# The up projections of a feed-forward layer by seven products of half blocks, in a phase of their own, in a tuned Trainium2 kernel

## The chip, the cores and the metric

The kernel runs on one core of one Trainium2 chip, in one launch. Its time is the device time of that core in microseconds (us), and less is better. The core has a tensor engine (PE, with its weight loads as PEld), VectorE (DVE), ScalarE (ACT), GpSimd (POOL) and a queue engine that issues loads (SP); each works through its own instructions in order and waits for the others by semaphores.

## The reference

One layer of a hybrid backbone on 640 tokens (128 of a prompt, 512 latent) of 2048 features, in float32: four groups of mixers behind a common input projection, an output projection, then a gated feed-forward part of 5632 = 44 x 128 features. The change touches that last part and the modulation ahead of it:

```python
def modulation(cond, w_ada, b_ada):
    m = jax.nn.silu(cond) @ w_ada + b_ada
    return jnp.split(m[:, None, :], N_MOD, axis=-1)

def ffn_sublayer(x, shift, scale, gate, g_pre, g_post, w1, w3, w2):
    h = modulate(rms_norm(x, g_pre), shift, scale)
    y = (jax.nn.silu(h @ w1) * (h @ w3)) @ w2
    return x + gate * rms_norm(y, g_post)
```

## The kernel before

Every large product is made in float32 precision from three float32r products: each operand is split into a rounded part (hi, or Rh, gh) and the rest (lo, or Rl, gl), and hi x hi, hi x lo and lo x hi are summed in PSUM. The input's parts Rh and Rl stay resident, 16 feature blocks by 640 tokens each. Weights come through the class `Stream` (lines 40 to 130): loads of 512 KB into four `raw` buffers on the SP queue run ahead, ScalarE makes the hi part of each half load (L101), VectorE the lo part (L102), both ahead of the products, as far as `part` buffers allow.

The order of all engines is the order in which the program is written: lists of steps (`p_c0`, `p_c1`, `p_wo`, `p_x`, `p_y`, `ff`) are run one after the other, and generators in `fillers` (norms, attention, the chains of the norm ahead of the feed-forward) are advanced by one piece after each step. From the end of the output projection on (tile `wo`, steps `p_wo`):

- `chain_a(t)` finishes the residual of a tile of 128 tokens (`mix`), writes it to DRAM (`x2d`), squares it and makes the diagonal `dg`; `chain_b(t)` transposes it by 16 products with `dg` (tile `tp`), scales and shifts it on ScalarE (L1261) and splits it into Rh and Rl. Three tiles' chains run among the last steps of the output projection, two among the first up products.
- `ff1_step(f, which, kh)` makes an up product for one block of 128 features and one of the weights w1 and w3: per block k of the 16, three passes, each in a matmul of 384 columns (tile `h_...X`) and one of 256 (`h_...Y`) with the weight part stationary (`gemm_b`). For w1 a silu follows on ScalarE, for w3 the multiply on VectorE and the split of the gated block into `gh`, `gl`.
- `ff2_step(c, n, kg)` makes the down product of a chunk of four blocks (11 chunks) for 512 output features: per block and token tile three matmuls of 512 columns with `gh` or `gl` stationary (tile `f`, in the last half chunk `f2l`), then a sum into `acc` (L1035).
- `gate_steps` makes the gates' modulation rows from 32 loads of 512 KB each (tile `gate`, 32 stationary columns): the first set among the input projection, the second threaded among the up products, in bursts of two blocks.

The list `ff` alternates: the first up products of chunk c, the down product of chunk c-1, the other up products of c. After the last chunk `final(t)` norms and writes each tile.

## Time and profile before

| | |
|---|---|
| time, median of 3 runs | 2931.72 us (2927.12 to 2933.48) |
| span of the profiled execution, first to last instruction | 2919.9 us (11.8 under that median; the rest of its own time lies around the span) |
| busy: PE, PEld | 97%, 86% |
| busy: DVE, ACT, POOL | 39%, 30%, 9% |
| mean granted clock of the tensor engine | 0.987 of full speed |
| moved by DMA | 357.99 MB, mean 123 GB/s |

Shares are means over stages with different limits. Matmuls overlap each other, so a matmul's own duration is longer than its share of the tensor engine: the distance from one start to the next is what it costs there. Clocks are given as a part of full speed; 1.00 is 2.4 GHz and 0.50 is 1.2 GHz.

### The profile page before, as it was taken

The page shows a single profiled execution, that of the slowest core. Times are in us where ns is not written, and L with a number is a line of the kernel's source. Part 1 is how long each engine was busy: PE and PEld are TensorE (multiplying, and loading weights), DVE is VectorE, ACT ScalarE, POOL GpSimd, SP SyncE. Part 2 cuts the span into 40 slices and gives each one's busy share as a digit, 9 for nine tenths or more (in the row PEclk, how much of TensorE's full clock was granted, in tenths as well). Part 3 has the DMA queues.
Part 4 walks back from the last instruction along what each step waited for, and adds up shares of the span by engine and source line. Part 5 has one row for each costly group of instructions (what it writes and reads, how often), then busy time and mean ns, then how long its engine had stood idle before and what let it go on. Part 6 is the DMA issues. An engine that isn't in the chain of part 4 may idle for free.

```text
span 2919.9 us, 41605 instructions
## 1 busy us (share of the span) xinstructions
PE 2820.1 (97%) x17244; PEld 2511.4 (86%) x17244; DVE 1147.4 (39%) x1974; ACT 866.6 (30%) x1787; POOL 255.2 (9%) x305
## 2 busy tenths in 40 slices
PE   5999999799999999999999999999999999999997
PEld 3888787678788899898999989899898989989895
DVE  4338955355524842223232232323323232232326
ACT  3235535244423742321221212122121122212124
POOL 0107811210000210000000000000000000000004
PEclk8999999899999999999999999999999999999998
DMA  7965554644333732222222222222222222222224
GB/s 294 317 223 174 191 194 140 124 160 164 115 105 128 253 125 80 86 89 73 102 73 87 87 87 91 76 94 80 87 87 80 94 77 90 87 73 75 77 73 195
DMA packets 103262, 357.99 MB, mean 123 GB/s; under 512 B 12240, under 2 KB 12496, under 8 KB 101408
## 3 DMA queue, kind: packets, MB, share of 16 engines
q1 hardware_dynamic: 94496, 320.38, 32.5%
q0 software_dynamic: 8144, 34.65, 3.4%
q8 instruction: 135, 2.21, 0.3%
q14 instruction: 55, 0.45, 0.0%
q10 hardware_dynamic: 432, 0.30, 0.0%
HBM read 336.37 MB, written 18.91 MB: 122 GB/s over the span
## 4 chain that ended last, share of the span: by engine, by line
PE 71%; DVE 2%; ACT 1%; issue 0%; POOL 0%; DVEq 0%; ACTq 0%
PE f L152 20%; PE wo L152 7%; PE gate L152 1%; PE h_18X L152 1%; PE h_26X L152 1%; PE h_22X L152 1%; PE h_34X L152 1%; PE h_6X L152 1%; PE h_14X L152 1%; PE h_30X L152 1%; PE h_10X L152 1%; PE h_13X L152 1%; PE h_17X L152 1%; PE h_21X L152 1%; PE h_33X L152 1%; PE h_29X L152 1%
## 5 line engine op out<-in xcount | busy, mean ns | idle before, releaser
L102 DVE TENSOR_TENSOR lo<-raw,hi 128x512 fp32r<-128x512 f32 (+1 forms) x800 | 554.9, 699 | 1490.0 <-ACT hi L101 1471.5
L101 ACT CAST hi<-raw 128x512 fp32r<-128x512 f32 (+1 forms) x800 | 477.1, 604 | 1494.5 <-PE f L152 424.9
L152 PE MATMUL f<-lo,gh 128*128 128x512 f32 x840 | 331.8, 395 | 0.0
L152 PE MATMUL f<-hi,gh 128*128 128x512 f32 x840 | 331.8, 395 | 0.0
L152 PE MATMUL f<-hi,gl 128*128 128x512 f32 x840 | 331.8, 395 | 0.0
L152 PEld LDWEIGHTS f<-hi,gl 128*128 128x128 f32 x840 | 157.7, 188 | 38.3
L152 PEld LDWEIGHTS f<-lo,gh 128*128 128x128 f32 x840 | 157.7, 188 | 37.9
L152 PEld LDWEIGHTS f<-hi,gh 128*128 128x128 f32 x840 | 157.7, 188 | 37.8
L357 POOL DMA_DIRECT2D gd<-gm x4 | 2.3, 589 | 1451.7 <-DVE gm L354 1451.7
L152 PE MATMUL wo<-hi,RhG 128*128 128x512 f32 x320 | 128.0, 400 | 0.0
L152 PE MATMUL wo<-lo,RhG 128*128 128x512 f32 x320 | 126.7, 396 | 0.7 <-DVE lo L102 0.7
L152 PE MATMUL wo<-hi,RlG 128*128 128x512 f32 x320 | 126.8, 396 | 0.0
L668 POOL TENSOR_TENSOR side<-side,tap 128x116 f32<-128x116 f32 (+19 forms) x140 | 115.3, 835 | 60.6 <-ACT tap L666 53.5
L1035 DVE TENSOR_TENSOR acc<-f,acc 128x512 f32<-128x512 f32 x190 | 117.1, 679 | 0.0
L152 PE MATMUL ada<-raw,cs 128*32 128x256 f32 x1024 | 75.8, 413 | 24.8 <-DMA raw<-in_w_mod_dram 24.7
L662 DVE SCALAR_TENSOR_TENSOR cm<-u,vec,cm 128x497 f32<-128x497 f32 (+14 forms) x100 | 92.4, 924 | 7.2 <-ACT cm L654 5.1
L1018 ACT CAST gh<-si 128x640 fp32r<-128x640 f32 x44 | 32.1, 729 | 171.2 <-DVE si L1015 171.2
L152 PEld LDWEIGHTS ada<-raw,cs 128*32 128x32 f32 x1024 | 27.1, 113 | 55.0 <-ACT sq L1165 19.5
L152 PEld LDWEIGHTS wo<-lo,RhG 128*128 128x128 f32 x320 | 60.2, 188 | 15.2 <-DVE lo L102 1.2
L152 PEld LDWEIGHTS wo<-hi,RhG 128*128 128x128 f32 x320 | 60.2, 188 | 14.3 <-issue 0.4
L152 PEld LDWEIGHTS wo<-hi,RlG 128*128 128x128 f32 x320 | 60.1, 188 | 14.3
L666 ACT ACTIVATE tap<-u,vec 128x116 f32<-128x116 f32 (+19 forms) x140 | 57.1, 436 | 23.1 <-POOL side L668 21.5
(1618 smaller groups left out, 7109.8 us busy)
## 6 DMA issues: line engine op xcount, KB each, us to landing
raw<-in_w_dram SPq DMA_DIRECT2D x272, 512.0 KB, 3.6
raw<-in_w_mod_dram SPq DMA_DIRECT2D x128, 512.0 KB, 5.2
raw<-in_w_gate_dram SPq DMA_DIRECT2D x64, 512.0 KB, 3.3
raw<-in_w_in_dram SPq DMA_DIRECT2D x64, 384.0 KB, 3.7
raw<-in_w_out_dram SPq DMA_DIRECT2D x48, 512.0 KB, 3.3
raw<-in_w_in_dram SPq DMA_DIRECT2D x16, 512.0 KB, 7.6
ud<-u POOLq DMA_DIRECT2D x24, 320.0 KB, 7.8
u<-ud SPq DMA_DIRECT2D x24, 320.0 KB, 4.2
```

Of the source, the lines that this page charges most:

```text
L101: self.nc.scalar.copy(hi[:, 0:n], t)
L102: self.nc.vector.tensor_tensor(out=lo[:, 0:n], in0=t, in1=f32(hi[:, 0:n]), op=ALU.subtract)
L152: nc.tensor.matmul(out=out, lhsT=lhsT, rhs=rhs, start=start, stop=stop)
L357: nc.gpsimd.dma_start(out=gd[row, cond].rearrange("(q x) -> q x", q=4), in_=dst[cond:P:32, :])
L662: nc.vector.scalar_tensor_tensor(out=o[:, so], in0=x[:, si], scalar=w[:, 15 + d:16 + d], in1=o[:, so], op0=ALU.mult, op1=ALU.add)
L666: nc.scalar.activation(out=t[:, 0:m - abs(d)], in_=x[:, si], func=AF.Copy, scale=w[:, 15 + d:16 + d])
L668: nc.gpsimd.tensor_tensor(out=side[:, so], in0=side[:, so], in1=t[:, 0:m - abs(d)], op=ALU.add)
L1018: nc.scalar.copy(gh[f], s)
L1035: nc.vector.tensor_tensor(out=acc[t][:, cc], in0=b, in1=acc[t][:, cc], op=ALU.add)
```

## The change

The up projections, 640 tokens x 2048 features x 256 output features at a time (a pair p of feature blocks, for w1 and then w3: 44 units), are written as products of 2 x 2 blocks: tokens in two halves of 320 (`TH`), the 16 feature blocks in even and odd ones (eight each, `KP`), the two output blocks. Strassen's seven products (`NP`) replace the eight: `TOKENS` and `WEIGHTS` say which blocks are added or subtracted for each. The sums of the tokens are made and split once (`ch`, `cl`, resident), those of the weights for each unit (`weight_sum`, `weight_low`), each product is 24 matmuls of 320 columns into a bank `m`, and `gather` adds it into the quadrants of the result. The up products run in a loop of their own, with the parts made two products ahead. The gated pair is written to DRAM (`ggd`); the down products, in chunks of 8, 8, 8, 8, 8 and 4 blocks, read it back and split it there (`g_load`, `g_split`). The chains of the norm now leave the scaled tokens unsplit in two tiles, `hal[0]` ("ha") and `hal[1]` ("hb"); once the token sums are made, parts of hb hold weight blocks and a result. The second set of gates is made between the output projection and the up phase, and each gate item covers 256 columns of all four row groups.

```diff
-CF = 4
-NC = NFF // CF
+TH = T // 2
+KP = KD // 2
+CHUNKS = (8, 8, 8, 8, 8, 4)
+NC = len(CHUNKS)
...
+    ggd = dram.tile([NFF // 2, P, 2, T], F32, name="ggd")
...
-        return (a["w_gate"][m // 3, half, k], (1024,), False)
+        return (a["w_gate"][m // 3, half, k], (4, 256), False)
...
-                for j in range(2):
-                    q = 2 * half + j
-                    mm(b[32 * q:32 * q + 32, :], cs[:, k, :], g[:, 512 * j:512 * j + 512],
-                       k % burst == 0, k % burst == burst - 1)
+                for q in range(4):
+                    mm(b[32 * q:32 * q + 32, 0:256], cs[:, k, :], g[:, q, :], k == 0, k == KD - 1)
...
-        return [one(k, half) for k in range(KD) for half in range(2)]
+        return [one(k, half) for half in range(2) for k in range(KD)]
...
-    def ff1_step(f, which, kh, part="XY"):
...
+    NP = 7
+    TOKENS = (((0, 0), (1, 1), ALU.add), ((0, 1), (1, 1), ALU.subtract), ((0, 0), None, None),
+              ((1, 0), (0, 0), ALU.subtract), ((0, 0), (0, 1), ALU.add), ((1, 1), None, None),
+              ((1, 0), (1, 1), ALU.add))
+    WEIGHTS = (((0, 0), (1, 1), ALU.add, False), ((1, 0), (1, 1), ALU.add, False), ((0, 1), (1, 1), ALU.subtract, False),
+               ((0, 1), (0, 0), ALU.add, True), ((1, 1), None, None, True), ((1, 0), (0, 0), ALU.subtract, True),
+               ((0, 0), None, None, True))
+    BLOCKS = ((0, 0), (1, 1), (1, 0), (0, 1))
...
+    N_W, N_HI = 5, 3
...
+    def load_weights(upto=None):
+        while at["load"] < min(4 * len(units), upto or 9999):
+            if upto is None and len(room["extra"]) + min(room["most"] - room["plain"], N_W - room["w"]) < 2:
+                return
+            u_, b_ = divmod(at["load"], 4)
+            p, wh = units[u_]
+            kf = BLOCKS[b_]
+            got = slot(f"B{kf[0] + 1}{kf[1] + 1}_{wh}_{p}", own=upto is not None and kf[1] == 0)
+            assert got is not None, "no room for a block"
+            nc.sync.dma_start(out=got[0], in_=(w1 if wh == 0 else w3)[p, kf[0], kf[1]])
+            raw[u_, kf] = got
+            at["load"] += 1
...
+    def weight_sum(s):
+        u_, i = divmod(s, NP)
+        x, y, op, last = WEIGHTS[i]
+        for kf in (x, y):
+            if kf is not None and (u_, kf) not in raw:
+                load_weights()
+                assert (u_, kf) in raw, ("no room for a block", s, room, list(raw))
+        bx = raw[u_, x]
+        t = bx
+        if y is not None:
+            if not last:
+                t = slot(f"t{i}_{u_}")
+                assert t is not None, "no room for a sum"
+            nc.vector.tensor_tensor(out=t[0], in0=bx[0], in1=raw[u_, y][0], op=op)
+        if last:
+            raw.pop((u_, x))
+        hi = slot(f"hi{i}_{u_}", F32R, "hi")
+        nc.scalar.copy(hi[0], t[0])
+        half[s] = (t, hi)
...
+    def weight_low(s):
+        t, hi = half.pop(s)
+        u_, i = divmod(s, NP)
+        lo = slot(f"lo{i}_{u_}", F32R)
+        assert lo is not None, "no room for a part"
+        nc.vector.tensor_tensor(out=lo[0], in0=t[0], in1=f32(hi[0]), op=ALU.subtract)
+        give(t)
+        held[s] = (hi, lo)
...
+    def product(s):
+        u_, i = divmod(s, NP)
+        hi, lo = held.pop(s)
+        b = bk[u_, i] = bank(f"m{i}_{u_}")
+        o = b[:, 0:TH]
+        for j in range(KP):
+            mm(o, hi[0][:, j, :], ch[i][:, j, :], j == 0, False)
+            mm(o, hi[0][:, j, :], cl[i][:, j, :], False, False)
+        for j in range(KP):
+            mm(o, lo[0][:, j, :], ch[i][:, j, :], False, j == KP - 1)
+        give(lo)
+        give(hi)
...
+    def gather(s):
+        u_, i = divmod(s, NP)
+        p, wh = units[u_]
+        c = cs_[wh]
+        c11, c12, c21, c22 = c[:, 0, 0:TH], c[:, 1, 0:TH], c[:, 0, TH:T], c[:, 1, TH:T]
+        b = bk.pop((u_, i))[:, 0:TH]
+        def plus(o):
+            nc.vector.tensor_tensor(out=o, in0=b, in1=o, op=ALU.add)
+        def minus(o):
+            nc.vector.scalar_tensor_tensor(out=o, in0=b, scalar=-1.0, in1=o, op0=ALU.mult, op1=ALU.add)
+        if i == 0:
+            nc.scalar.copy(c22, b)
+            nc.scalar.copy(c11, b)
+        elif i == 1:
+            plus(c11)
+        elif i == 2:
+            nc.scalar.copy(c12, b)
+            plus(c22)
+        elif i == 3:
+            plus(c22)
+        elif i == 4:
+            plus(c12)
+            minus(c11)
+        elif i == 5:
+            plus(c11)
+            nc.scalar.copy(c21, b)
+        else:
+            plus(c21)
+            minus(c22)
+            if wh == 0:
+                nc.scalar.activation(out=c, in_=c, func=AF.Silu)
+            else:
+                nc.vector.tensor_tensor(out=c, in0=c, in1=cs_[0], op=ALU.mult)
+                nc.gpsimd.dma_start(out=ggd[p], in_=c)
...
+    def token_sums(i):
+        x, y, op = TOKENS[i]
+        blk = lambda q, t, k: hal[t][:, 4 * q + k:4 * q + 4:2, :]
+        srcs = []
+        for q in range(4):
+            qs = slice(2 * q, 2 * q + 2)
+            src, got = blk(q, *x), None
+            if y is not None:
+                got = slot(f"ts{i}_{q}")
+                v = got[0].rearrange("p a b -> p (a b)")[:, 0:2 * TH].rearrange("p (a b) -> p a b", a=2)
+                nc.vector.tensor_tensor(out=v, in0=src, in1=blk(q, *y), op=op)
+                src = v
+            nc.scalar.copy(ch[i][:, qs, :], src)
+            srcs.append((qs, src, got))
+            if q:
+                token_low(i, *srcs[q - 1])
+        token_low(i, *srcs[3])
+    def token_low(i, qs, src, got):
+        nc.vector.tensor_tensor(out=cl[i][:, qs, :], in0=src, in1=f32(ch[i])[:, qs, :], op=ALU.subtract)
+        if got is not None:
+            give(got)
...
+    def g_load(p):
+        if p < NFF // 2:
+            r = pools["x"].tile([P, 2, T], F32, tag="graw", name=f"graw{p}", bufs=2)
+            nc.gpsimd.dma_start(out=r, in_=ggd[p])
+            gh["raw", p] = r
+    def g_split(p):
+        r = gh.pop(("raw", p))
+        for e in range(2):
+            f = 2 * p + e
+            gh[f] = pools["g"].tile([P, T], F32R, tag="gh", name=f"gh{f}")
+            gl[f] = pools["g"].tile([P, T], F32R, tag="gl", name=f"gl{f}")
+            nc.scalar.copy(gh[f], r[:, e, :])
+            nc.vector.tensor_tensor(out=gl[f], in0=r[:, e, :], in1=f32(gh[f]), op=ALU.subtract)
...
+                    if lo_ < hi_:
+                        nc.scalar.activation(out=hal[h][:, k, lo_ - h * TH:hi_ - h * TH],
+                                             in_=b[:, j * P + lo_ - t * P:j * P + hi_ - t * P], func=AF.Identity,
+                                             scale=S2[:, k, cond:cond + 1], bias=H2[:, k, cond:cond + 1])
...
+    def chains_ab():
+        for kind, t in ((0, 3), (1, 0), (1, 1), (0, 4), (1, 2), (1, 3), (1, 4)):
+            yield from (chain_b if kind else chain_a)(t)
...
+    rlctx.close()
+    rhctx.close()
+    h1p, h1_ctx = scope("h1p", side="right")
+    hal[1] = h1p.tile([P, KD, TH], F32, name="hb")
+    h0p, h0_ctx = scope("h0p", side="right")
+    hal[0] = h0p.tile([P, KD, TH], F32, name="ha")
+    fillers.append(chains_ab())
+    for e in p_g2:
+        e()
+        advance()
     drain()
     part_ctx.close()
     x_ctx.close()
+    wctx.close()
...
+    n = NP * len(units)
+    def up(s_):
+        if s_ + 2 < n:
+            weight_sum(s_ + 2)
+        if s_:
+            gather(s_ - 1)
+        if s_ + 2 < n:
+            weight_low(s_ + 2)
+        product(s_)
+    load_weights(4)
+    token_sums(0)
+    weight_sum(0)
+    weight_low(0)
+    token_sums(1)
+    weight_sum(1)
+    weight_low(1)
+    for s_ in range(NP):
+        i = s_ + 2
...
+        if i < NP:
+            token_sums(i)
+        if i == 6:
...
+        up(s_)
+        if i >= 6:
+            load_weights()
+    for s_ in range(NP, n):
+        up(s_)
+        load_weights()
+    gather(n - 1)
...
+    ff = [add([ff2_step(c, n, kg) for n in range(4) for kg in range(CHUNKS[c] // 2)]) for c in range(NC)]
+    st2.ahead = 4
+    st2.load()
+    more["n"] = 0
+    g_load(0)
+    g_load(1)
+    for p in range(CHUNKS[0] // 2):
+        g_split(p)
+        g_load(p + 2)
+    for c in range(NC - 1):
+        todo = list(range(F0[c + 1] // 2, (F0[c + 1] + CHUNKS[c + 1]) // 2)) if c + 1 < NC - 1 else []
+        for i, e in enumerate(ff[c]):
+            e()
+            if todo and i % 3 == 2:
+                p = todo.pop(0)
+                g_split(p)
+                g_load(p + 2)
...
+    pools["g"], g_ctx = scope("gq", 4)
+    for p in range(F0[NC - 1] // 2, NFF // 2):
+        g_split(p)
+        g_load(p + 2)
...
-    o["w1"] = A["ffn_w1"][0].reshape(16, 128, 44, 128).transpose(2, 1, 0, 3)
-    o["w3"] = A["ffn_w3"][0].reshape(16, 128, 44, 128).transpose(2, 1, 0, 3)
+    blocks = lambda w: w.reshape(8, 2, 128, 22, 2, 128).transpose(3, 1, 4, 2, 0, 5)
+    o["w1"] = blocks(A["ffn_w1"][0])
+    o["w3"] = blocks(A["ffn_w3"][0])
```

Within the up phase the tensor engine had, for block 9 of w1 or w3, rows of 384 and 256 columns with both token parts:

```order
L152 MATMUL h_9X<-RhG_92,hi_12547 128x384
L152 MATMUL h_9Y<-RhG_92,hi_12547 128x256
L152 MATMUL h_9X<-RlG_96,hi_12547 128x384
L152 MATMUL h_9Y<-RlG_96,hi_12547 128x256
L152 MATMUL h_9X<-RhG_92,lo_12548 128x384
L152 MATMUL h_9Y<-RhG_92,lo_12548 128x256
```

Now it has the end of one product of a unit (rows of 320 columns with ch and cl in turn, then eight with the lo part) and the start of the next:

```order
L157 MATMUL m_23_15350<-ch_9817,hi_23_15281 128x320
L157 MATMUL m_23_15350<-cl_9818,hi_23_15281 128x320
L157 MATMUL m_23_15350<-ch_9817,lo_23_15284 128x320 x8
L157 MATMUL m_23_15384<-ch_9999,hi_23_15313 128x320
L157 MATMUL m_23_15384<-cl_10000,hi_23_15313 128x320
```

The two halves of unequal width became products of one width, of which a unit has seven. On VectorE the stretch before held the multiply and split of a gated block and the lo parts of loads:

```order
L1014 TENSOR_TENSOR si_12983<-h_10X,si_12983 128x384
L1015 TENSOR_TENSOR si_12983<-h_10Y,si_12983 128x256
L1019 TENSOR_TENSOR gl_13111<-si_12983,gh_13110 128x640
L102 TENSOR_TENSOR lo_13117<-raw_12929,hi_13116 128x512
L102 TENSOR_TENSOR lo_13147<-raw_13050,hi_13146 128x512
```

Now, around the end of a unit for w3 and the start of the next for w1 (t: a weight sum, lo: its low part, m into hb: the gather, 128x1280: the multiply with silu's result):

```order
L1094 SCALAR_TENSOR_TENSOR hb<-m_17_13973,hb 128x320
L1065 TENSOR_TENSOR lo_18_14005<-t_18_13999,hi_18_14001 128x1024
L1053 TENSOR_TENSOR t_18_14032<-hb 128x1024
L1091 TENSOR_TENSOR hb<-m_17_14007,hb 128x320
L1065 TENSOR_TENSOR lo_18_14038<-t_18_14032,hi_18_14034 128x1024
L1053 TENSOR_TENSOR t_18_14065<-hb 128x1024
L1091 TENSOR_TENSOR hb<-m_17_14040,hb 128x320
L1094 SCALAR_TENSOR_TENSOR hb<-m_17_14040,hb 128x320
L1118 TENSOR_TENSOR hb<-hb,c_9822 128x1280
L1065 TENSOR_TENSOR lo_18_14073<-t_18_14065,hi_18_14067 128x1024
```

Sums of weights and of products came in between the lo parts, each of which is twice as wide. The gates, on the tensor engine, stood alone between steps of the up products:

```order
L152 MATMUL h_11X<-RhG_95,lo_13117 128x384
L152 MATMUL h_11Y<-RhG_95,lo_13117 128x256
L152 MATMUL gate_2_12671<-raw_12992,cs 32x512 x2
L152 MATMUL h_11X<-RhG_92,hi_13146 128x384
L152 MATMUL h_11Y<-RhG_92,hi_13146 128x256
L152 MATMUL h_11X<-RlG_96,hi_13146 128x384
```

Now they follow the last row of the output projection, and the transposing products of the chains stand between them:

```order
L157 MATMUL wo_4_9160<-hi_9259,RlG_100 128x512
L157 MATMUL gate_0_9323<-raw_9197,cs 32x256 x4
L157 MATMUL gate_0_9323<-raw_9219,cs 32x256 x4
L157 MATMUL gate_0_9323<-raw_9241,cs 32x256 x4
L157 MATMUL gate_0_9323<-raw_9263,cs 32x256 x4
L157 MATMUL tp_0_9391<-dg_8917,mix_7982 128x128 x4
L157 MATMUL gate_0_9323<-raw_9345,cs 32x256 x4
```

The chains' rows and the gates' rows moved together, with no large products among them. ScalarE, ahead of the first down products, had silu and split of a block among the hi casts of weights:

```order
L1009 ACTIVATE si_10267<-h_2X 128x384
L1010 ACTIVATE si_10267<-h_2Y 128x256
L101 CAST hi_10272<-raw_10079 128x512
L101 CAST hi_10302<-raw_10113 128x512
L101 CAST hi_10330<-raw_10113 128x512
L101 CAST hi_10360<-raw_10155 128x512
L1018 CAST gh_10390<-si_10267 128x640
```

Now it goes from the last gather of the up phase through the eight casts of chunk 0's gated blocks (read back into graw) to the first cast of w2:

```order
L1111 COPY hb<-m_43_19963 128x320
L1161 CAST gh_20048<-graw_20044 128x640
L1161 CAST gh_20052<-graw_20044 128x640
L1161 CAST gh_20058<-graw_20046 128x640
L1161 CAST gh_20062<-graw_20046 128x640
L1161 CAST gh_20068<-graw_20056 128x640
L1161 CAST gh_20072<-graw_20056 128x640
L1161 CAST gh_20078<-graw_20066 128x640
L1161 CAST gh_20082<-graw_20066 128x640
L103 CAST hi_20088<-raw_20036 128x512
L103 CAST hi_20092<-raw_20036 128x512
```

The casts of the gated blocks moved out from among the weights' casts to a place ahead of them all.

## Rows read from the trace of the kernel before

**Rows 1.** The page's first part: busy time of each engine, its share of the span, instructions.
```profile
PE 2820.1 (97%) x17244; PEld 2511.4 (86%) x17244; DVE 1147.4 (39%) x1974; ACT 866.6 (30%) x1787; POOL 255.2 (9%) x305
```
**Rows 2.** Busy time by stretch, from the first up product to the last down product: length, then busy us and instructions of each engine, granted clock, share and rate of DMA.
```profile
1001.16:2901.21 1900.05, 1899.85 (x11281) 1746.24 (x11279) 601.91 (x976) 438.78 (x796) 39.88 (x37) 1.00 0.26 91
```
**Rows 3.** The timeline of the tensor engine within an up product (start, duration, engine, line, operation), and one row of the view of tile h_0Y: its weight loads, min/median/max ns.
```profile
1400.07 0.34 PE L152 MATMUL h_9X<-RhG,hi 128*128 128x384 f32 x1
1400.25 0.28 PE L152 MATMUL h_9Y<-RhG,hi 128*128 128x256 f32 x1
1400.36 0.34 PE L152 MATMUL h_9X<-RlG,hi 128*128 128x384 f32 x1
...
1407.40 0.34 PE L152 MATMUL h_9X<-RlG,hi 128*128 128x384 f32 x1
...
L152 PEld LDWEIGHTS h_0Y<-RhG,hi x32: 187/188/192, 1041.7 to 1053.1; 128*128 128x128 f32 x32
```
**Rows 4.** The same timeline in the output projection: 63 matmuls from the first row to the second, then a group of transposing products.
```profile
943.64 0.40 PE L152 MATMUL wo<-hi,RlG 128*128 128x512 f32 x1
...
958.35 0.40 PE L152 MATMUL wo<-hi,RlG 128*128 128x512 f32 x1
958.58 1.05 PE L152 MATMUL tp<-dg,mix 128*128 128x128 f32 x8
959.39 0.48 PE L152 MATMUL wo<-hi,RhG 128*128 128x512 f32 x1
```
**Rows 5.** The same timeline around a gate item among the up products, and four modulation items of 256 columns behind each other in an early stage (32 records).
```profile
1407.87 0.28 PE L152 MATMUL h_9Y<-RhG,lo 128*128 128x256 f32 x1
1408.08 1.05 PE L152 MATMUL gate<-raw,cs 128*32 128x512 f32 x4
1409.06 0.45 PE L152 MATMUL h_10X<-RhG,hi 128*128 128x384 f32 x1
1409.35 0.28 PE L152 MATMUL h_10Y<-RhG,hi 128*128 128x256 f32 x1
...
60.37 1.93 PE L152 MATMUL ada<-raw,cs 128*32 128x256 f32 x32
```
**Rows 6.** The early stage in which modulation items wait for their loads: the timeline, and the busy time of its stretch (columns as in rows 2).
```profile
45.06 1.08 PE L152 MATMUL ada<-raw,cs 128*32 128x256 f32 x8 [0.20 <-DMA raw<-in_w_mod_dram]
...
50.95 0.69 PE L152 MATMUL w3a<-RhG,hi 128*128 128x384 f32 x1 [3.57 <-ACT hi L101]
...
51.65 0.52 PE L152 MATMUL w3a<-RlG,hi 128*128 128x384 f32 x1
...
52.18 0.52 PE L152 MATMUL w3a<-RhG,lo 128*128 128x384 f32 x1
...
54.73 0.28 PE L152 MATMUL w3b<-RhG,lo 128*128 128x256 f32 x1
...
40.00:50.00 10.00, 5.02 (x34) 1.10 (x34) 2.82 (x10) 1.06 (x2) 0.00 (x0) 0.50 1.01 384
```
**Rows 7.** Groups of VectorE's instructions by shape (busy us, mean ns, idle time before them), and two rows of the views of tiles h_0X and h_0Y: reads of PSUM, min/median/max ns.
```profile
L102 DVE TENSOR_TENSOR lo<-raw,hi 128x512 fp32r<-128x512 f32 x672 | 463.4, 695 | 1341.8 <-ACT hi L101 1334.4 <-PE w5a L152 6.8
L1019 DVE TENSOR_TENSOR gl<-si,gh 128x640 fp32r<-128x640 f32 x44 | 36.3, 825 | 35.0 <-ACT gh L1018 35.0
...
L1014 DVE TENSOR_TENSOR si<-h_0X,si x1: 548/548/548, 1054.0 to 1054.0; 128x384 f32<-128x384 f32 x1
L1015 DVE TENSOR_TENSOR si<-h_0Y,si x1: 412/412/412, 1054.4 to 1054.4; 128x256 f32<-128x256 f32 x1
```
**Rows 8.** Groups of ScalarE's instructions by shape (as rows 7), and its reads of PSUM from the views of tiles h_0X and h_0Y.
```profile
L101 ACT CAST hi<-raw 128x512 fp32r<-128x512 f32 x672 | 413.3, 623 | 1309.3 <-PE f L152 424.9 <-PE wo L152 111.6 <-DMA raw<-in_w_in_dram 76.1
L1018 ACT CAST gh<-si 128x640 fp32r<-128x640 f32 x44 | 32.1, 729 | 171.2 <-DVE si L1015 171.2
L1261 ACT ACTIVATE tm<-tp,H,S 128x128 f32<-128x128 f32 x80 | 30.7, 496 | 4.9 <-PE tp L152 2.5 <-issue 1.5 <-ACT hi L101 1.0
...
L1240 ACT ACTIVATE jm<-mix 128x512 f32<-128x512 f32 x20 | 12.6, 632 | 9.7 <-DVE mix L1231 9.7
...
L190 ACT ACT_TABLE_LOAD x4 | 5.1, 1283 | 0.1
...
L1240 ACT ACTIVATION_READ_ACCUMULATOR jm<-mix 128x1 f32 x20 | 3.7, 186 | 0.0
...
L1009 ACT ACTIVATE si<-h_0X x1: 491/491/491, 1050.8 to 1050.8; 128x384 f32<-128x384 f32 x1
L1010 ACT ACTIVATE si<-h_0Y x1: 378/378/378, 1051.2 to 1051.2; 128x256 f32<-128x256 f32 x1
```
**Rows 9.** The stretch with the highest DMA rate (columns as in rows 2), and DMA issues by tile: count, KB each, median us from issue to landing.
```profile
10.00:20.00 10.00, 0.47 (x8) 0.23 (x8) 8.89 (x11) 9.54 (x14) 0.00 (x0) 1.00 1.02 398
...
raw<-in_w_dram SPq DMA_DIRECT2D x272, 512.0 KB, 3.6
raw<-in_w_mod_dram SPq DMA_DIRECT2D x128, 512.0 KB, 5.2
...
ud<-u POOLq DMA_DIRECT2D x24, 320.0 KB, 7.8
...
x2d<-mix POOLq DMA_DIRECT2D x5, 1024.0 KB, 7.2
x<-x2d POOLq DMA_DIRECT2D x5, 1024.0 KB, 17.7
```

More of the change, by code (lines that the diff above doesn't have):

```diff
@@ new lines, in backbone, with slot @@
+    BLOCKS = ((0, 0), (1, 1), (1, 0), (0, 1))
+    ch, cl, hal = [None] * NP, [None] * NP, [None, None]
+    units = [(p, wh) for p in range(NFF // 2) for wh in range(2)]
+    raw, half, held, cs_, bk = {}, {}, {}, {}, {}
+    N_W, N_HI = 5, 3
+    room = {"w": 0, "hi": 0, "plain": 0, "most": 2, "extra": []}
+    at = {"load": 0}
+    def slot(name, dt=F32, tag="w", own=False):
+        if dt == F32 and room["extra"] and not own:
+            return room["extra"].pop(0), "extra"
+        most = N_W if tag == "w" else N_HI
+        if room[tag] >= most or (dt == F32 and room["plain"] >= room["most"]):
+            return None
+        room[tag] += 1
+        room["plain"] += dt == F32
+        return pools["w"].tile([P, KP, P], dt, tag=tag, name=name, bufs=most), ("plain" if dt == F32 else tag)
@@ new lines, in token_low @@
+    def token_low(i, qs, src, got):
+        nc.vector.tensor_tensor(out=cl[i][:, qs, :], in0=src, in1=f32(ch[i])[:, qs, :], op=ALU.subtract)
+        if got is not None:
+            give(got)
+    gh, gl, acc, late, gated = {}, {}, {}, [], {}
+    F0 = [sum(CHUNKS[:c]) for c in range(NC)]
+    def g_load(p):
[3 more added lines that the diff above has]
+            gh["raw", p] = r
```

197 lines of the change are left out of this document (90 added, 107 removed).

## The prediction

> **What bounds the kernel now.** I read the page first for the shares, then the stretch from the first up product to the last down product, and then single matmuls for their cadence. The tensor engine is busy 97% of the span [rows 1]; in the stretch that the change rebuilds, 1001.16 to 2901.21 us, it is busy 1899.85 of 1900.05 us at the full granted clock (1.00, that is 2.4 GHz), while VectorE has 601.9 us of work and ScalarE 438.8 [rows 2]. So this stretch ends when its matmuls are done, and only fewer streamed columns, or an idle tensor engine, can move it. The price of a column: 25 steps from one 384-wide matmul of h_9X to the same of a later pair take 1407.40 - 1400.07 = 7.33 us, 293.2 ns for each pair of 384 and 256 columns, 0.458 ns a column [rows 3]. The 512-wide ones go at (958.35 - 943.64) / 63 = 233.5 ns, 0.456 ns a column [rows 4]. It is a price by column at 256, 384 and 512 alike.
>
> **The up products.** Before: 44 features x 2 weights x 16 blocks x 3 passes = 4224 pairs x 0.2932 = 1238.5 us. After: 44 units (22 feature pairs x 2 weights) x 7 products x 24 matmuls of 320 columns = 7392. No row shows 320; it lies between 256 and 384, so 320 x 0.458 = 146.6 ns (by the 512-wide rate 145.9), 3.52 us a product, 24.63 us a unit, 1083.7 us in all. Taken alone that is -154.8 us; the other end would be 145.9 ns, 5 us more gain.
>
> The Trainium skill, page "TensorE: Matmul & The Clock Gate", section "Back-to-back issue gap", gives N / 2.4 + 2.5 ns for the warm spacing. By it a pair would take 271.7 ns against the 293.2 of rows 3, a 320-wide one 135.8, and the saving would be an estimated 143.6 us. The trace does not agree with the rule here, and the sum goes by the rows.
>
> **Can the other engines feed it?** The splits (hi, lo) had two engines far from full; now each unit asks more of them. VectorE, by its rows of 512 (695 ns) and 640 (825 ns) [rows 7], costs 1.016 ns more for each further element: 1.215 us for 1024, 1.475 for 1280. The reads of PSUM took 548 at 384 and 412 at 256, so 0.48 at 320. A unit has 5 weight sums and 7 lo parts (12 x 1.215 = 14.6), 8 sums into the output quadrants (3.8) and, in every second one, a 1280-wide multiply (0.7 a unit): 19.2 us of 24.6. ScalarE, from 623 at 512 and 729 at 640 [rows 8]: 1.05 us for each of 7 casts, 4 copies at 0.43, half a silu: about 9.7. Order on VectorE is sum (s+2), gather (s-1), lo (s+2): it waits for the end of product s-1, then has gather and lo to do, 1.7 to 2.2 us, and has them done some 2.5 us after that end, while product s+2 begins 7 us after it. The longest run (two gathers, multiply, lo, sum: 4.9 us) eats 1.4 of that and is paid back at the next product, whose gather has no VectorE work. Loads: 2 MB a unit in 24.6 us, each issued two or three products before its sum; a 512 KB load lands in 3.6 to 5.2 us [rows 9]. The tightest, block (0,1), has about 7 us. The write of the gated tile is POOL's only work; its space is written again a unit later, and such writes land in 7 to 8 us [rows 9]. So I put the steady phase at the matmuls' own pace, and nothing on it for the round trip through DRAM.
>
> **The gate stage.** The second half of the gates was threaded among the up products; now its 32 loads of 512 KB, 20 groups of four transposing products (tp) and the norm chains stand between the output projection and the up phase, alone. Three things run beside each other. DMA: 28 loads after the four that are prefetched; the best window moved 398 GB/s [rows 9], 1.32 us each, 37 us, and some 3.6 MB beside them (two tiles of x2d, one of x, the gates' rows), 9 us: 46. ScalarE: 64 scalings at 30.7 / 80 = 0.38 [rows 8], 32 shorter ones for the tile that the halves split, about 0.33, eight squares at 0.82 with their accumulator reads, some 4 us of roots and of tables at 1.28: 46. TensorE: a gate item of 4 x 256 columns has the form of the ada items, 32 records in 1.93 us, 0.48 an item [rows 5]; tp groups cost 0.81 [rows 4]: 16 + 16, and 52 changes between the two at some 0.2 (a gate among the up products starts 0.21 after the last of them, where 0.12 is usual, and the second one behind it comes at 0.29 for 0.18): 42. But where ada items waited for loads before, the clock stood at 0.50 (1.2 GHz) and one took 1.08 us [rows 6]; at that level the stage would be 32 x 1.08 + 20 x 1.62 = 67. The ends are 46 and 77 with a first chain of some 6 to 10; I take 58, nearer to the first, since a tensor engine that is full with tp and gates has work without pause. Given back: the 12 tp groups that leave the output projection, 0.9 each, 10.8.
>
> **The entry.** After the last tp, VectorE works alone: token sums, 5 of 8 x 0.825 and 2 of 4 x 0.825 (39.6); 5 weight sums and 7 lo parts (14.6); gathers (1.5); five round trips to ScalarE for hi, with about 4.8 idle. That is 60.5 us, under which unit 0's seven products lie. Unit 1's blocks can be loaded only when the last token sum has read hb, at about 58.8, and land at 64; its sum and cast end at 66.3, when its first product can start. So unit 0 takes 66 us in place of 24.6. Were all of ScalarE's part hidden it would be 58; with later loads 80.
>
> **The turn to the down products.** ScalarE and VectorE have all four splits of chunk 0 ahead of the first split of w2, and these hang on a chain: last gathers and multiply 2.7, the write to DRAM and its wait some 7, first read landing at about 9, two splits (0.73 and 0.82 each half), and then two more reads through two buffers, each 5 to 6 us: about 21. From below 12 (one read, as if only gated tile 0 were needed), from above 33 (reads of x back from x2d took 17.7 us to land [rows 9]). Cover there is none: the down products need them.
>
> **The rest.** 2640 down matmuls stay at 0.2335, 616.4. Fewer sums into acc (six chunks for eleven) lie beside them and save nothing. Two starts at the low clock: behind a pause the products ran at the low level from 50.95 to 54.73 [rows 6], which lost half of that, so 2 each, 4. The last chunk's lo split behind its last sum, 2. The first gates, now on four column groups at once, save half of 0.98 on items that stood alone [rows 5], about a third of 32, in a stretch where VectorE is busy beside them: 0 to 5, I take 2.
>
> **Sum**, for the 1900.05 us stretch: -10.8 + 58 + 66.3 + 43 x 24.63 (1059.1) + 21 + 616.4 + 4 + 2 = 1816.0, so -84.1, and -2 for the first gates: -86. The profiled span of 2919.9 becomes 2833.8; the median of the times is 11.8 above the span, and keeping that it is 2931.7 - 86 = 2846.
>
> **Rivals.**
> - The stages outside the products are dear: gates at the low clock (77), entry 80, turn 33: +45, 2891. For it speaks the clock of 0.50 in rows 6.
> - They are cheap: gates 46, entry 58, turn 12: -29, 2817.
> - Slower: the loop gather, sum, hi, lo comes late by some microseconds in each product, so that the tensor engine pauses before it and the clock falls. A pair at 0.50 took 52.18 - 51.65 = 0.53 us [rows 6], a product then 6.36 instead of 3.52, +2.84. From 30 such products of 301 on nothing is left of the gain; with a quarter of them it is +213, 3059. Against it: 5 us of VectorE's 24.6 are free and parts are made two products ahead.
> - The change doesn't do what it says, for a 320-wide matmul is paced by its weight load, 188 ns in the records [rows 3]: 7392 x 0.188 = 1389.7, 306 more: 3152. Against it: the 256-wide ones follow at 117 ns in rows 3 beside loads of the same 188.
>
> On the third: the Trainium skill, same page, section "HAM oscillation — how this bites in real kernels", tells of pauses between bursts that bring back the half clock each time. The trace agrees with the fall in rows 6 (0.50).
>
> **How the numbers follow.** Forecast 2846 (2822 to 2872): 0.70. Cheap stages: 0.09. Dear stages: 0.12. Slower by the loop: 0.07. Load-bound: 0.02. The range 2812 to 2888 holds the forecast, most of the cheap case and most of the dear one, 0.8 to 0.85. Within 0.2% (2926 to 2938, about what a measurement of this kernel can tell from no change) falls only a thin part of the third rival: 0.01. Faster 0.90, slower 0.09.
>
> **What would show it.** In the profile after: matmuls of m spaced 146 to 147 ns and 24.6 us from one unit's first product to the next, VectorE near 78% there; the stretch from the last wo to the first m near 58, from there to unit 1 near 66, from the last m to the first f near 21; 1.00 of clock in the up phase. Spacing of 188 would make the fourth rival right, gaps before each product the third, and a gap of over 30 in any of the three stages the first.

## The result, and the profile after

The changed kernel takes 2846.47 us (median, 2843.96 to 2848.19), the kernel before 2931.95 beside it: ratio 0.9714, 95% interval 0.9697 to 0.9731, 85.5 us less. The forecast was 2846. The profiled span is 2846.4, though, where the sum had 2833.8, so the steps have to be looked at one by one.

The busy time by stretch, columns as in [rows 2]: up to the output projection, that projection, the gate stage to the last gate row, from there to the first product of unit 1, units 1 to 43, the turn, the down products, the tail.

```profile
0.00:767.20 767.20, 678.34 (x5019) 573.71 (x5019) 422.68 (x769) 316.69 (x747) 185.62 (x235) 0.96 0.60 193
767.20:1005.94 238.74, 232.94 (x982) 184.66 (x978) 102.96 (x192) 90.30 (x187) 13.86 (x26) 0.99 0.42 146
1005.94:1065.69 59.75, 43.34 (x417) 25.84 (x416) 12.42 (x42) 39.97 (x120) 5.35 (x10) 0.94 0.90 328
1065.69:1128.48 62.79, 34.91 (x170) 33.33 (x169) 55.63 (x70) 28.62 (x39) 1.15 (x2) 0.76 0.13 49
1128.48:2188.28 1059.80, 1059.80 (x7226) 1059.70 (x7224) 793.72 (x880) 396.98 (x496) 11.23 (x21) 1.00 0.28 99
2188.28:2208.91 20.63, 0.17 (x2) 0.00 (x0) 8.16 (x11) 5.98 (x10) 3.17 (x6) 0.58 0.53 181
2208.91:2832.15 623.24, 619.70 (x2640) 497.48 (x2640) 225.74 (x355) 160.60 (x278) 35.41 (x39) 0.99 0.30 106
2832.15:2846.40 14.25, 0.17 (x1) 0.00 (x0) 9.15 (x20) 3.71 (x8) 6.52 (x5) 0.66 0.40 161
```

| us | before | forecast | after | off by |
|---|---|---|---|---|
| up to the first row of the output projection | 760.7 | 758.7 | 767.2 | +8.5 |
| output projection | 240.5 | 229.7 | 238.7 | +9.1 |
| gate stage | - | 58 | 59.8 | +1.8 |
| entry, to unit 1's first product | - | 66.3 | 62.8 | -3.5 |
| units 1 to 43 | - | 1059.1 | 1059.8 | +0.7 |
| turn | - | 21 | 20.6 | -0.4 |
| down products (with 4 + 2 for clock and last chunk) | - | 622.4 | 623.2 | +0.8 |
| tail | 18.7 | 18.7 | 14.3 | -4.4 |

From the first row of the output projection on it is 2159.2 before and 2079.2 after: -80.0 where the sum had -84.1. The large term holds to 0.1%: the tensor engine is busy 1059.80 of 1059.80 us at 1.00, and the timeline of two products there (answers to [rows 3]) has 15 steps in 1503.90 - 1501.70 = 2.20 us, 146.7 ns:

```profile
1500.52 1.34 PE L157 MATMUL m<-ch,lo 128*128 128x320 f32 x8
1501.70 0.31 PE L157 MATMUL m<-ch,hi 128*128 128x320 f32 x1
...
1503.90 0.31 PE L157 MATMUL m<-cl,hi 128*128 128x320 f32 x1
1504.04 0.75 PE L157 MATMUL m<-ch,lo 128*128 128x320 f32 x4
```

The output projection gave back 1.7 of the 10.8 us. The tensor engine's timeline (answers to [rows 4]) stops there again and again from 965 to 978 for weight parts, and behind these pauses it goes on at the low clock until 983; the last line is the busy time of that stretch, columns as above, with a granted clock of 0.51:

```profile
964.98 0.40 PE L157 MATMUL wo<-hi,RhG 128*128 128x512 f32 x1
966.23 0.50 PE L157 MATMUL wo<-lo,RhG 128*128 128x512 f32 x1 [0.85 <-DVE lo L104]
...
967.26 0.40 PE L157 MATMUL wo<-hi,RlG 128*128 128x512 f32 x1
968.87 0.50 PE L157 MATMUL wo<-hi,RhG 128*128 128x512 f32 x1 [1.22 <-ACT hi L103]
...
978.13 0.80 PE L157 MATMUL wo<-hi,RhG 128*128 128x512 f32 x1 [0.94 <-ACT hi L103]
...
980.30 0.63 PE L157 MATMUL wo<-lo,RhG 128*128 128x512 f32 x1
980.73 0.63 PE L157 MATMUL wo<-hi,RlG 128*128 128x512 f32 x1
...
976.30:983.30 7.00, 6.05 (x15) 3.94 (x14) 5.17 (x15) 5.51 (x13) 1.61 (x3) 0.51 0.87 282
```

Of the 9.1 us that it was off, 5.8 are idle tensor engine (238.74 - 232.94); most of the rest are products that came every 0.43 us instead of every 0.23.

In the gate stage the tensor engine's longer pauses end with a load (two of them here, beside [rows 5]); then it has no work until the first token and weight sums are made:

```profile
1025.32 0.64 PE L157 MATMUL gate<-raw,cs 128*32 128x256 f32 x8 [1.95 <-DMA raw<-in_w_gate_dram]
...
1043.54 0.64 PE L157 MATMUL gate<-raw,cs 128*32 128x256 f32 x8 [1.97 <-DMA raw<-in_w_gate_dram]
...
1075.13 0.63 PE L157 MATMUL m<-ch,hi 128*128 128x320 f32 x1 [9.43 <-ACT hi L1057]
```

And the turn is the chain of reads that was forecast, on ScalarE's timeline (casts of gated blocks, then of w2):

```profile
2197.22 2.84 ACT L1161 CAST gh<-graw 128x640 fp32r<-128x640 f32 x4 [11.31 <-DMA graw<-ggd]
2203.87 1.35 ACT L1161 CAST gh<-graw 128x640 fp32r<-128x640 f32 x2 [3.81 <-DMA graw<-ggd]
2206.99 1.35 ACT L1161 CAST gh<-graw 128x640 fp32r<-128x640 f32 x2 [1.77 <-DMA graw<-ggd]
2208.25 2.17 ACT L103 CAST hi<-raw 128x512 fp32r<-128x512 f32 x4
```

### The profile page after: what moved, and what is told of

It reads as the page before. It is cut to its first block, busy times and chain, and to the rows that moved or that the text cites. A ratio compares the mean times of both kernels' runs of the same rounds, so it can differ in the third digit from the quotient of the medians.

```text
span 2846.4 us, 40521 instructions
## 1 busy us (share of the span) xinstructions
PE 2669.4 (94%) x16444; PEld 2374.7 (83%) x16444; DVE 1630.5 (57%) x2335; ACT 1042.8 (37%) x1881; POOL 262.3 (9%) x343
## 4 chain that ended last, share of the span: by engine, by line
issue 35%; PE 23%; DVE 2%; POOL 0%; ACT 0%; DMA 0%; DVEq 0%; POOLq 0%; ACTq 0%
PE f L157 20%; PE m L157 3%; POOL ggd L1119 0%; DVE acc L1178 0%; DMA graw<-ggd 0%; DVE acc L1236 0%; DVE gt L1187 0%; DVE lo L104 0%; ACT jf L1181 0%; DVE gl L1162 0%; ACT hi L103 0%; DVE cl L1141 0%; DVE hb L1118 0%; DVE ts L1132 0%; PE f2l L157 0%
## 5 line engine op out<-in xcount | busy, mean ns | idle before, releaser
L157 PE MATMUL m<-ch,hi 128*128 128x320 f32 x2464 | 734.0, 311 | 27.9 <-ACT hi L1057 27.9
L157 PE MATMUL m<-cl,hi 128*128 128x320 f32 x2464 | 732.7, 311 | 0.0
L104 DVE TENSOR_TENSOR lo<-raw,hi 128x512 fp32r<-128x512 f32 (+1 forms) x432 | 303.5, 711 | 739.8 <-ACT hi L103 739.2
L103 ACT CAST hi<-raw 128x512 fp32r<-128x512 f32 (+1 forms) x432 | 249.0, 587 | 819.4 <-PE f L157 437.5
L157 PEld LDWEIGHTS m<-ch,hi 128*128 128x128 f32 x2464 | 466.6, 189 | 30.3 <-ACT hi L1057 30.3
L157 PEld LDWEIGHTS m<-cl,hi 128*128 128x128 f32 x2464 | 467.0, 190 | 0.0
L157 PE MATMUL m<-ch,lo 128*128 128x320 f32 x2464 | 412.7, 310 | 0.0
L157 PEld LDWEIGHTS m<-ch,lo 128*128 128x128 f32 x2464 | 375.8, 189 | 0.0
L1065 DVE TENSOR_TENSOR lo<-hb,hi 128x1024 fp32r<-128x1024 f32 x129 | 157.2, 1219 | 25.0 <-ACT hi L1057 25.0
L1065 DVE TENSOR_TENSOR lo<-t,hi 128x1024 fp32r<-128x1024 f32 x129 | 157.5, 1221 | 24.4 <-ACT hi L1057 22.3
```

The lines of the kernel that those rows point to most:

```text
L103: self.nc.scalar.copy(hi[:, 0:n], t)
L104: self.nc.vector.tensor_tensor(out=lo[:, 0:n], in0=t, in1=f32(hi[:, 0:n]), op=ALU.subtract)
L157: nc.tensor.matmul(out=out, lhsT=lhsT, rhs=rhs, start=start, stop=stop)
L1065: nc.vector.tensor_tensor(out=lo[0], in0=t[0], in1=f32(hi[0]), op=ALU.subtract)
```

## The experiments

Each is one profiled execution, unless rounds are told. The part ahead of the output projection is the same code in all changed kernels, but took 764.5 to 779.1 us in these runs, so kernels are compared from the first row of the output projection to the end ("the rest": 2079.2 in the changed kernel).

### The kernel before, once more

No edit.

> The kernel before, unchanged, profiled again. The sum of the prediction kept 11.8 us around the span of 2919.9. Theory 1: that span was of an execution some 10 us faster than the median, and what lies around a span is about 1.8 us, as in the four runs of the changed kernel; then the span comes out between 2925 and 2932, 1.8 under its own time, and the stretch ahead of the first row of the output projection (760.7 before, 767.2 after) is longer than 760.7. Theory 2: 11.8 us is a constant around this kernel's span; then the span is again 2918 to 2922 with a time near 2932.

Span 2936.2, 1.8 under its own time of 2938.0; the median in ten runs was 2939.99, ratio 1.0006 (0.9996 to 1.0017).

```profile
0.00:776.99 776.99, 682.89 (x4890) 573.12 (x4890) 420.25 (x767) 316.33 (x747) 185.58 (x233) 0.95 0.60 190
1017.46:2917.50 1900.04, 1899.84 (x11280) 1746.31 (x11279) 601.95 (x976) 438.79 (x796) 39.88 (x37) 1.00 0.27 91
```

Theory 1 holds in kind (the span was above the range): the up and down stretch is the same to 0.01 us as in [rows 2], what follows the first row of the output projection is again 2159.2, and the difference is all in the first part, 777.0 for 760.7. So 10 of the 11.8 us of the prediction were no overhead but an execution with a short first part. The time was the median less 86, so this step moved only the predicted span; and of the first part's +8.5, or the 2 us hoped for from the first gates, nothing can be told.

### How much room the up phase has

```diff
         for j in range(KP):
             mm(o, hi[0][:, j, :], ch[i][:, j, :], j == 0, False)
-            mm(o, hi[0][:, j, :], cl[i][:, j, :], False, False)
-        for j in range(KP):
-            mm(o, lo[0][:, j, :], ch[i][:, j, :], False, j == KP - 1)
+            mm(o, hi[0][:, j, :], cl[i][:, j, :], False, j == KP - 1)
```

> The changed kernel with the third pass (lo part of the weights) left out of each of the 308 products, so 16 matmuls in place of 24; all other engines do what they did. Theory 1 (the up phase ends with its matmuls, and VectorE, 781.1 us busy in 1043.0, is the next limit): a unit falls from 24.65 to VectorE's 18.5 to 20, not to the 16.4 of its matmuls; span 2846 - 44 x 5 = some 2620. Rival (the round of gather, sum, hi and lo is nearly as long as a product, so the phase has little left): a unit stays above 21.5, span above 2700.

The span is 2741.0, and a unit takes 22.1 on average (21.6 and 22.7 in turn). So the rival holds: not VectorE's load, 756.88 busy of 929.28 us, stops it, but a loop. Its timeline, in which a sum waits for the lo part ahead of it, that for ScalarE's hi, and that for the sum:

```profile
1505.06 1.22 DVE L1053 TENSOR_TENSOR t<-B,hb 128x1024 f32<-128x1024 f32 x1
...
1507.46 1.23 DVE L1065 TENSOR_TENSOR lo<-t,hi 128x1024 fp32r<-128x1024 f32 x1 [0.39 <-ACT hi L1057]
1508.60 1.22 DVE L1053 TENSOR_TENSOR t<-hb 128x1024 f32<-128x1024 f32 x1
...
1511.00 1.23 DVE L1065 TENSOR_TENSOR lo<-t,hi 128x1024 fp32r<-128x1024 f32 x1 [0.79 <-ACT hi L1057]
1512.15 1.22 DVE L1053 TENSOR_TENSOR t<-hb 128x1024 f32<-128x1024 f32 x1
```

One round is 1512.15 - 1508.60 = 3.55 us, as long as a product of 24 matmuls (3.52); the products without a sum make up for it. The unit's loop is 22.1 of 24.65: the prediction's third rival was 10% away, not the 22% by VectorE's busy time.

### The output projection

```diff
-            yield from chain_a(t)
+            for _ in chain_a(t):
+                yield
+                yield
+                yield
```

> The changed kernel with the chains of tiles 0 to 2 advanced one piece at every third chance instead of at each, among the last steps of the output projection. Theory 1 (three chains back to back keep ScalarE and VectorE from splitting weights ahead, which stops the tensor engine from 965 to 983): the output projection falls from 238.5 to about 229.5 us, the rest stays. Rival (the two engines have too much work in these 45 us whatever the order): it stays above 235.

The projection takes 228.3 (238.5 from first row to last row in the changed kernel), the rest 2067.1, 12 less. Theory 1 holds, and beside the 240.5 of the kernel before 11.9 us are given back (its tensor engine is busy 228.58 of 228.58 us, at a clock of 1.00): the 10.8 was about the right price. Three chains in a row made a cycle of 9.26 us (ScalarE's first square at 955.74, 965.00 and 974.26) with three half loads split in each; three halves give 18 matmuls, 4.2 us of work. Before, groups of transposing products stood between the chains [rows 4], and the splits had caught up.

### The turn

The layout takes the read-back tiles and the split blocks from the space of the token sums, the first two reads go to the SP queue, and pairs 2 and 3 are split later:

```diff
-            r = pools["x"].tile([P, 2, T], F32, tag="graw", name=f"graw{p}", bufs=2)
-            nc.gpsimd.dma_start(out=r, in_=ggd[p])
+            r = grp.tile([P, 2, T], F32, tag="graw", name=f"graw{p}", bufs=2)
+            (nc.sync if p < 2 else nc.gpsimd).dma_start(out=r, in_=ggd[p])
...
-    pools["x"], f_ctx = scope("fp")
-    pools["g"], g_ctx = scope("gp", 16, side="right")
+    grp, gr_ctx = scope("grp", 2)
+    pools["g"], g_ctx = scope("gp", 16)
+    pools["x"], f_ctx = scope("fp", side="right")
...
-    for p in range(CHUNKS[0] // 2):
+    for p in range(2):
         g_split(p)
         g_load(p + 2)
...
             e()
+            if c == 0 and i < 2:
+                g_split(i + 2)
+                g_load(i + 4)
```

> The changed kernel with the space of the read-back tiles and of the split blocks taken from the token sums instead of the weights and results, the first two reads on the SP queue, and pairs 2 and 3 of the first chunk split after the first two down steps. Theory 1 (the 20.6 us between the last up product and the first down product are a chain of late reads through two buffers): it falls to 4 to 8 us, span down by 13 to 16. Rival (the first splits wait for the last write and for the end of the last unit's products whatever is done): 11 to 14 us stay, span down by 7 to 9.

The turn takes 6.0 us, 14.6 less, as theory 1 had it. But the rest fell by 31.7, to 2047.5: 15.2 us came off the down products, which nobody had expected. They came every 226.7 ns in place of 233.3. The next run has the order without the layout and the SP queue (the last two pieces of that diff), and another edit in the gate stage (`kq` counts banks of four blocks):

```diff
-                    if lo_ < hi_:
+                    if lo_ < hi_ and kq % 2:
+                        nc.vector.tensor_scalar(out=hal[h][:, k, lo_ - h * TH:hi_ - h * TH],
...
+                    elif lo_ < hi_:
                         nc.scalar.activation(out=hal[h][:, k, lo_ - h * TH:hi_ - h * TH],
```

> The changed kernel with two edits in stages that don't meet. First, only the order of the shorter turn, without its layout: pairs 2 and 3 of the first chunk are split after the first two down steps. Theory 1 for the turn (two of the three reads in a row go, the wait for the last products' space stays): 20.6 falls to 10 to 12.5; rival (the order did all of it): to 6 to 7. The cadence of the down products stays at 233.3 if the layout sets it, and falls to 226.7 if the order did. Second, VectorE takes the scalings of every second bank of four blocks, so that the two engines don't wait for each other as they did with every second scaling. Theory 1 for the gate stage (the gates' loads set it): the last gate row comes 56 to 59 after the output projection, 59.4 before; rival (ScalarE sets it): 50 or less.

The turn took 12.5, at the upper end of theory 1's range, and the down products 233.3 ns: some 8 us of the turn are the order, 6.5 the space and the SP queue together, which no run takes apart, and the cadence belongs to the layout. The last gate row came 57.5 us after the last row of the output projection, where the changed kernel has 59.4, so theory 1 holds for the gate stage. Not even the 1.9 are a gain that is shown: in the four other runs that leave this stage and the projection's chains alone (two passes, the turn, the sums, the operands' place) it came at 57.0 to 60.2.

### The gate stage

Every second scaling on VectorE (the diff above with `j % 2`):

> The changed kernel with every second scaling behind the transposing products (the step from tp to ha and hb) on VectorE instead of ScalarE. Between the last row of the output projection and the last gate row lie 59.75 us in the profile, with ScalarE busy some 42 of them and the tensor engine waiting for gate loads. Theory 1 (the loads set the stage: 28 of them and some 3.6 MB beside them at about 390 GB/s): it shrinks by 0 to 6 us. Rival (ScalarE's chain of squares and scalings sets it): it shrinks by 10 to 15.

The last gate row came at 58.3 (59.4 in the changed kernel), the rest was 2077.8. It is theory 1's number, but this run can't speak for it: by the timelines of the same edit without gates (two runs further down) the engines took turns, since readers of one bank were made to wait for each other:

```profile
1020.62 0.81 ACT L1395 ACTIVATE ha<-tp,H,S 128x128 f32<-128x128 f32 x2 [1.29 <-DVE ha L1390]
1021.11 0.76 DVE L1390 TENSOR_SCALAR ha<-tp,S,H 128x128 f32<-128x128 f32 x2 [0.53 <-ACT ha L1395]
...
1021.90 0.81 ACT L1395 ACTIVATE ha<-tp,H,S 128x128 f32<-128x128 f32 x2 [0.48 <-DVE ha L1390]
1022.40 0.76 DVE L1390 TENSOR_SCALAR ha<-tp,S,H 128x128 f32<-128x128 f32 x2 [0.53 <-ACT ha L1395]
```

The gates moved among the down products (`merge` puts one item behind each step):

```diff
-    p_g2 = add(gate_steps(5, gm2, 1))
...
-    for e in p_g2:
-        e()
-        advance()
     drain()
...
+        ff.append(add(merge(main, g2[16 * c - 16:16 * c] if c in (1, 2) else [])))
```

> The changed kernel with the second set of gates (32 loads, 32 items) taken out of its stage and put among the down products of the second and third chunk, one item behind each step. Theory 1 (the loads set the stage, and VectorE's token sums stand behind the row of the last gates, though the last scaled tile is there at 1058.3, 7.5 us before): the time from the last row of the output projection to the first up product, 69.2, falls to 50 to 55, by ScalarE's work; the two chunks of down products grow by 32 x 0.57 to 0.8 = 18 to 26, so the span changes by +6 to -2. Rival (the norm chains with their squares and roots set the stage and the loads are under them): 69.2 falls by no more than 8, and the span grows by over 10.

From the output projection's last row to the first up product: 52.2 for 69.4, as theory 1 had it; so the gates, with their loads, are worth 17 us of the stage. The down products grew by 24.2, 0.76 an item, and the rest is 2085.4, 6.2 more, at the edge of what theory 1 allowed: what was idle tensor engine beside the chains became time of its own.

> Both of the last two edits: no gates in the stage, and every second scaling on VectorE. Theory 1 (without the loads ScalarE's scalings are what is left): the time from the last row of the output projection to the first up product falls by another 8 to 12 beside the run with the gates moved alone, to 40 to 46. Rival (the chain of sum, root, product, square and root of the last two tiles is what is left): less than 4 lower.

52.5: no gain, so theory 1's number fails. The edit itself is why: the two engines waited for each other, as shown above. It says nothing on the chain.

### The entry

```diff
-                nc.vector.tensor_tensor(out=v, in0=src, in1=blk(q, *y), op=op)
+                nc.gpsimd.tensor_tensor(out=v, in0=src, in1=blk(q, *y), op=op)
```

> The changed kernel with the additions of the token sums (20 of 640 elements) on GpSimd instead of VectorE. By the profile 62.8 us lie between the last gate row and the first product of unit 1, in which VectorE is busy nearly without a pause. Theory 1 (VectorE alone sets the entry): the 20 additions, 16.5 us, leave it; GpSimd needs some 2.2 us each by its products of 512 (1.74), 8.7 a sum, and the entry falls to 46 to 52. Rival (the two engines slow each other, or GpSimd's 8.7 a sum set a new bound): it stays at 57 or more.

From the start of the last gate row to unit 1's first product it took 71.7, where the changed kernel, counted in this way, has 63.4: the rival, and dearer. By groups (busy us, mean ns), first the changed kernel's from 1060 to 1135:

```profile
L1141 DVE TENSOR_TENSOR cl<-ex,ch 128x640 fp32r<-128x640 f32 x16 | 13.2, 822 | 0.5
```

and the same stretch of this run:

```profile
L1141 DVE TENSOR_TENSOR cl<-ex,ch 128x640 fp32r<-128x640 f32 x16 | 24.8, 1587 | 4.3 <-ACT ch L1134 3.8
...
L1132 POOL TENSOR_TENSOR ex<-ha 128x640 f32<-128x640 f32 x4 | 8.8, 2218 | 1.2 <-DVE lo L1065 1.2
```

VectorE's subtraction took twice its time (1587 for 822 ns) beside the additions. The Trainium skill, page "SBUF — State Buffer", section "SBUF: two separate sides", says that GpSimd and a VectorE instruction with two SBUF inputs exclude each other on one pair of ports; these rows agree in that they show the delay (1587 for 822 ns), though not the ports.

### Where the operands lie

In the shorter turn `gh` and `gl` had come to lie, by the allocation (the addresses that the program gives its tiles), at the same offset within 256 bytes of a partition as the weight parts. If that is it, 32 bytes ahead of everything on the left do the same in the changed kernel:

```diff
+    const.tile([P, 8], F32, name="pad")
     vec = const.tile([P, NV], F32, name="vec")
```

> The changed kernel with one unused tile of 32 bytes per partition ahead of the constants, and nothing else: all that is allocated from the left moves by 32 bytes, and what is allocated from the right (the stationary operands of the output projection and of the down products) stays. By the allocation the weight parts then lie at the same offset within 256 bytes as those operands; in the changed kernel they differ by 32, and in the run with the shorter turn, where the 512-wide down products came every 226.7 ns instead of 233.3, they were equal. Theory 1 (the relative place of the two operands sets the 6.6 ns): 512-wide products of the output projection and of the down phase both come every 226.7 ns, span down by 960 x 6.6 + 2640 x 6.6 ns = 24. Rival (something else in that run's layout or order did it): both stay at 233.

Theory 1 holds for both stages: the projection took 232.1 (238.5), the down products 606.6 (623.0), the rest 2057.7. The timeline of the down products in this run, and in the changed kernel:

```profile
2399.74 0.39 PE L157 MATMUL f<-lo,gh 128*128 128x512 f32 x1
...
2401.10 0.39 PE L157 MATMUL f<-lo,gh 128*128 128x512 f32 x1
```

```profile
2399.70 0.40 PE L157 MATMUL f<-hi,gl 128*128 128x512 f32 x1
...
2401.10 0.40 PE L157 MATMUL f<-hi,gl 128*128 128x512 f32 x1
```

Six steps each: 1.36 us against 1.40. One trace shows it too: by the allocation some 105 of the changed kernel's own down products have equal offsets, and they came every 226.8 ns, the others every 233.4. (In its last half chunk, where both kinds alternate, the equal ones took 231.3.) In the kernel before, `gh` and the parts of w2 differ by 128 bytes within 256:

```diff
     pools["x"], f_ctx = scope("fp")
+    pools["x"].tile([P, 32], F32, name="pad_f")
```

> The kernel before with one unused tile of 128 bytes per partition at the start of the pool that holds gh and gl, so that they lie at the same offset within 256 bytes (64) as the weight parts of w2 (they were 128 apart); nothing else. Theory 1 (equal offsets within 256 bytes end the slow cadence, in this kernel as in the changed one): the 2640 down products come every 226.7 ns in place of 233.5, the up products stay at 293.2 a pair, the span falls by 17 to 18, ratio 0.994. Rival (only a difference that is no multiple of 64 bytes is slow, and 128 is not): no change, ratio 1.000.

2919.41 for 2937.12 in three rounds, ratio 0.9941 (0.9925 to 0.9958); the down products come every 226.9 ns, as theory 1 had it. So this gain is not the change's: most of it could be had in the kernel before.

### Together

> What helped, in one kernel: the spread chains, the shorter turn with its layout, the scalings by bank on two engines, the tile of 32 bytes, and half of the second set of gates (16 of 32 items) among the down products of the second chunk. Expected of the span 2846.4, by stage: output projection -10, its cadence -6; the time to the first up product from 69 to 42 to 50, since 16 loads and the chains then end together, -19 to -27; turn -14; down products -17 for the cadence and +12 for the gates; sum -54 to -62, a span of 2784 to 2792 and a time of 2786 to 2802 with some 8 of difference in the early stages from run to run. If the loads were not what sets the stage, it stays above 60 and the time above 2798.

2793.69 (2789.70 to 2796.30, five runs), ratio 0.9516 (0.9503 to 0.9529) to the kernel before; span 2791.1, as expected, the rest 2016.2, which is 63 less than the changed kernel's. The output projection, the stage to the first up product, the turn and the down products with 16 gate items:

```profile
774.90:997.40 222.50, 222.50 (x982) 183.26 (x978) 102.24 (x192) 89.47 (x186) 13.86 (x26) 1.00 0.45 152
997.40:1039.00 41.60, 29.19 (x290) 21.63 (x289) 34.28 (x100) 27.23 (x77) 4.30 (x8) 0.92 0.83 309
...
2151.60:2157.90 6.30, 0.31 (x3) 0.05 (x2) 4.98 (x7) 3.32 (x6) 1.03 (x2) 0.79 0.76 308
2157.90:2776.30 618.40, 614.90 (x2768) 497.54 (x2768) 230.19 (x359) 163.27 (x281) 38.16 (x46) 1.00 0.36 123
```

The projection has no idle tensor engine left (222.50 of 222.50). With half of the gates in the stage and half below, the stage to the first up product takes 41.6 us, at +11.7 in the down products (618.3 against 606.6): 53.3 together, where all gates in the stage took 67.5 in the run of the order, which has the same scalings by bank. With none in the stage it was 52.2 + 24.2, but with all scalings on ScalarE; no run has none of the gates and the scalings by bank, so it is not shown that half is the best share.

## Why the prediction was right, step by step

- **Fewer columns.** 146.7 ns and 24.65 us a unit, as forecast; right. The reading behind it, one price by column up to 512, was wrong in part: 117 ns at 256 [rows 3] and 146.7 at 320 are both 0.458 a column, but 512 columns come every 226.7 ns, 0.443 a column, where the operands lie well. The 512-wide ones of [rows 4] had 6.8 ns on top and so seemed to fit; that this too comes from where their operands lie was tried on the changed kernel's output projection, not on that one. 320 lies between widths that had been read, so the forecast took no harm.
- **Other engines feed it.** Right, with less room than was said: VectorE is busy 75% there (78% forecast), but the limit beneath is the loop of sum, hi and lo, 22.1 of 24.65 us.
- **Gate stage, 58.** 59.8, and the loads pace it, as the run with none of the gates there shows. But 58 was picked between 46 and 77, and the term behind the 46 was too small: the stage moved 328 GB/s, not 398, and at that rate the prediction's own 18.3 MB (46 us x 398 GB/s) take 56 us. The pick was partly luck. The clock stayed at 0.94 in the mean, so the dear rival's first term did not come.
- **The 10.8 us given back by the output projection.** This term failed: 1.7 came, though 11.9 came once the chains were spread (the 0.81 a group of [rows 4] would make 9.7, not 10.8). The price was right and the overlap was not: the transposing products were taken as a pure cost there, but they also kept the chains apart, so that splits could run ahead.
- **Entry, 66.3.** 62.8: VectorE's work (55.63 busy and 7.2 idle, where the sum had 60.5 with 4.8 idle) decides by its rows, not the load behind the last token sum; the first load of unit 1 was issued at 1118.58, 52.9 us after the last gate row and not 58.8, before the last token sum's additions were done. No run confirms it: the one that took work off VectorE slowed it.
- **Turn, 21.** 20.6, by the chain as told (first read landed at 8.9, 9 forecast); the run with the shorter turn takes 14.6 of it away.
- **The sum.** +9.1 and the small terms against -4.4 in the tail, where the engines' last rows stand as before and only GpSimd's last drain behind them is shorter (10.2 us before, 5.8 after, by the traces; why is open), leave +4.1 in the rest. The medians differ by 85.5 and not by 80.0; the other 5.5 lie ahead of the output projection, if the profiled stages stand for all executions, and that is within what that part varies by. So that 2846 was met to 0.5 us is luck, two errors of some 4 us against each other; the stages that the change rebuilds are worth 80 us.

## What to carry to other kernels

Work that is taken out from between two bursts may have been what kept them apart: ask which engine runs ahead there, and count what it gets done in a burst. When a stage is left with one engine's loads and another engine's idle time, try to move a part of it, so that both end together. A phase at 100% of one engine can be a few per cent from a dependency loop that no busy time shows; leave out a pass and read the period.

## What was not expected of the hardware

- The 512-wide float32r products came every 226.7 ns where both operands lay at the same offset within 256 bytes of a partition, and every 233.3 to 233.5 where these differed by 32, 128 or 160. One unused tile of 32 bytes was worth 21.5 us here. The 320-wide products of one token sum, whose offset differs by 32, showed no such cost (3.52 to 3.53 us a product); what in the memory does it was not tried.
- GpSimd's additions doubled the time of VectorE's subtractions beside them (822 to 1587 ns).
- The part ahead of the output projection varied by some 15 us between executions of the same code (764.5 to 779.1 in the changed kernels, 760.7 to 777.0 in the kernel before), while stages that no edit touched came out the same to about 1 us, but for the gate stage (57.0 to 60.2).
